# The path for overfull experts: a run-time loop with transfers on SP becomes seven conditional blocks without SP

## The chip, the cores and the metric

The kernel runs on one core of a Trainium2 chip. The metric is the device time of one launch in microseconds (us). TensorE (PE) multiplies matrices and has its own queue of weight loads (PEld); VectorE (DVE), ScalarE (ACT) and GpSimd (POOL) do the rest; SyncE (SP) here does nothing but issue transfers from HBM to the on-chip memory. A letter q behind an engine's name (SPq) marks its sequencer: register loads, branches, semaphores, issues of transfers. A measurement of this kernel can tell about 0.2% from no change.

## The reference

A trunk of two layers over 256 tokens of width 1024. Each layer has a mixer half (normalisation, an mLSTM branch and a grouped-query attention branch, merged and projected) and a half with experts, all in float32. The change concerns the second half alone. Cut down:

```python
def hierarchical_moe(h, ...):                     # h: 256 tokens x 1024
    p_group = softmax(t @ w_rg + b_rg)            # 4 groups, the best one is taken
    p_top, g_idx = lax.top_k(p_group, 1)
    ...                                           # 8 experts in each group
    w_top, e_idx = lax.top_k(p_exp, TOP_K)        # the best two of the group
    w_top = w_top / jnp.sum(w_top, ...) * p_top
    combine = ...                                 # 256 x 32, two entries in each row
    for g in range(N_GROUPS):
        a = einsum('td,edf->tef', t, w_gate[sl])  # 1024 -> 512
        u = einsum('td,edf->tef', t, w_up[sl])
        act = silu(a) * u * combine[:, sl, None]
        out = out + einsum('tef,efd->td', act, w_down[sl])   # 512 -> 1024
```

The layer then adds `gate2 * out` to its tokens. A token uses two of the 32 experts, so an expert has 16 tokens on average, and how many each has is known only at run time.

## The kernel before, in words

`experts(l, ...)` does this half for layer `l`. Logits, the choice of experts and each token's place in its expert's list (`posm`) come first; `pp[:, 64:96]` holds the count of tokens of each expert. Each expert has 64 slots (`CAP`), and the experts are worked on as 16 pairs of 2 x 64 slots (loop over `i`, L1449).

For a pair, `onehot` (L1247) compares `posm` with the slot numbers, `weigh` (L1254, GpSimd) puts the weights in, `gather` (L1263) multiplies the tokens with the one-hot matrix, `gate_up` (L1294) runs gate and up, `act_mul` and `act_T` (L1307, L1311) form and turn the activations, `down` (L1317) multiplies with the down weights, `leave` (L1332) scales and splits the result into `yh` and `yl`, and `scatter` (L1339) adds it to the tokens `xs`. The scatter of a pair is done within the next pair.

All weights stream through a ring of slots in the on-chip memory. A gate, up or down matrix of a pair comes in two pieces of 2 MB (`pump`, L173 to L208: L194 and L196 issue one whole piece, L191 two halves of 1 MB). SP issues them in an order fixed when the program is built, each when its slot is free (TensorE has read what was in it) and a completion count is free. TensorE's and SP's order is that of the program text (`MANUAL`, L64); the small work on VectorE, ScalarE and GpSimd is put in order by a planner.

After pair 11 (`MIDDLE`) the kernel provides for experts with more than 64 tokens: `rest()` (L1414). All five engines load the largest count (L1415; it is written to `ci` by L1241 to L1243 in `weights()`) and compare it with 64 (L1417). Only if it is larger does a run-time loop over the 32 experts run, load each count, and for a full expert do `rest_block` (L1379) twice, for tokens 64 to 191 and from 192 on. `rest_block` gathers 128 tokens and loads the expert's weights in eight transfers from SP into `y` (L1396, L1406), the same tile that `leave` writes. With the inputs here no expert has more than 64 tokens. Behind the `if` the next pair's `onehot`, `gather` and `turn` follow (L1478 to L1480).

Of the kernel before, what the change touches and what calls it, by code (L numbers as in the profile page):

```python
# [10 lines left out]
F32 = mybir.dt.float32  # L11
I32 = mybir.dt.int32
F32R = mybir.dt.float32r
AF = mybir.ActivationFunctionType
ALU = mybir.AluOpType
AX = mybir.AxisListType.X
PSUM = bass.MemoryType.PSUM

P = 128
S = 256  # L20
D = 1024
NT = 2
# [4 lines left out]
NE = 32  # L27
# [6 lines left out]
CAP = 64  # L34
NPAIR = NE // 2
# [25 lines left out]

PK = {"cols": (0, 96), "br": (96, 36), "gb": (132, 16), "gqk": (148, 128), "b3": (276, 8), "wg8": (284, 256)}
NPK = 540
MANUAL = {mybir.EngineType.PE, mybir.EngineType.SP}  # L64


def trunk(ctx, tc, x, c, b_ada, b_in, mlstm_norm_g, norm2_g, final_g,
          rope, gate_t, up_t, down_t, tail_t, ada_t, in_t, branch_t, out_t, packs, router, out, dbg=None, depth=DEPTH):
    nc = tc.nc
    V, A, G, T = nc.vector, nc.scalar, nc.gpsimd, nc.tensor  # L70
# [3 lines left out]
    sm = ctx.enter_context(tc.tile_pool(name="sm", bufs=2))  # L74
# [199 lines left out]
    first = {}  # L274
# [52 lines left out]
    iot = cst.tile([P, P], F32, name="iot")  # L327
    desc = cst.tile([P, 8], F32, name="desc")
    whose = cst.tile([P, 2 * NE], I32, name="whose")
# [804 lines left out]
    def experts(l, p, pL, lc, ssn, xa, sh2c):  # L1134
# [3 lines left out]
        y = pool.tile([P, D], F32, name="y")  # L1138
# [11 lines left out]
        def small(nm, *shape):  # L1150
            n = 1
            for v in shape:
                n *= v
            o = used[0]
            used[0] += n
            assert used[0] <= 1760
            return at(10, o, *shape)
# [5 lines left out]
        for t in range(NT):  # L1163
# [4 lines left out]
            if t == 0:  # L1168
                V.scalar_tensor_tensor(xp[1][:, t], xa[:, t], r, xp[0][:, t].bitcast(F32), op0=ALU.mult,
                                       op1=ALU.subtract)  # L1170
# [38 lines left out]
        pp = ps.tile([P, 512], F32, tag="c", name="pp")  # L1209
        T.matmul(pp[:, 0:64], lhsT=trisb, rhs=mk.rearrange("p t g e -> p (t g e)"), start=True, stop=False)  # L1210
        T.matmul(pp[:, 32:64], lhsT=onesb, rhs=mkf[:, 0, :], start=False, stop=True)
        for t in range(NT):
            T.matmul(pp[:, 64:96], lhsT=onesb, rhs=mkf[:, t, :], start=t == 0, stop=t == 1)
        posm = small("posm", NT, NE)
        V.scalar_tensor_tensor(posm, pp[:, 0:64].rearrange("p (t e) -> p t e", t=NT), 1.0, mkf, op0=ALU.add,
                               op1=ALU.mult)
        V.tensor_scalar(posm, posm, -1.0, None, op0=ALU.add)

        cb = small("cb", NT, NE)
        ci = sm.tile([1, NE + 1], I32, tag="ci", name="ci", bufs=1)  # L1220

        def weights():
            eg = small("eg", NT, 4)
            V.tensor_tensor(eg, lg, gm_.unsqueeze(2).to_broadcast([P, NT, 4]), op=ALU.subtract)
            A.activation(eg, eg, AF.Exp)
            e2 = small("e2", NT, 4)
            V.tensor_tensor(e2, m2, m1, op=ALU.subtract)
            A.activation(e2, e2, AF.Exp)
            sg_ = small("sgs", NT)
            V.tensor_reduce(sg_, eg, axis=AX, op=ALU.add)  # L1230
            wa, wb = small("wa", NT, 4), small("wb", NT, 4)
            V.scalar_tensor_tensor(wa, e2, 1.0, sg_.unsqueeze(2).to_broadcast([P, NT, 4]), op0=ALU.add, op1=ALU.mult)
            V.reciprocal(wa, wa)
            V.tensor_tensor(wa, wa, oh4, op=ALU.mult)
            V.tensor_tensor(wb, wa, e2, op=ALU.mult)
            V.tensor_tensor(oh1, oh1, wa.unsqueeze(3).to_broadcast([P, NT, 4, 8]), op=ALU.mult)
            V.tensor_tensor(oh2, oh2, wb.unsqueeze(3).to_broadcast([P, NT, 4, 8]), op=ALU.mult)
            V.tensor_tensor(cb, oh1.rearrange("p t g e -> p t (g e)"), oh2.rearrange("p t g e -> p t (g e)"),
                            op=ALU.add)
            mxc = small("mxc", 1)  # L1240
            V.tensor_copy(ci[:, 0:NE], pp[0:1, 64:96])  # L1241
            V.tensor_reduce(mxc[0:1, :], pp[0:1, 64:96], axis=AX, op=ALU.max)
            V.tensor_copy(ci[:, NE:NE + 1], mxc[0:1, :])  # L1243

        marks = {}

# [33 lines left out]
        count = [0]  # L1280
# [95 lines left out]
                turn_rows(range(2, 4))  # L1376


        def rest_block(e, at_, base):  # L1379
            pe = small("pe", NT, 1)  # L1380
            V.tensor_scalar(pe, posm[:, :, ds(e, 1)], -float(base), None, op0=ALU.add)
            ce = small("ce", NT, 1)
            V.tensor_copy(ce, cb[:, :, ds(e, 1)])
            oh = slots_of.rearrange("p t e s -> p (t e s)")[:, 0:S].rearrange("p (t s) -> p t s", t=NT)
            ow = same("ow", 10, 0, 2, NT, P)
            for t in range(NT):
                V.tensor_scalar(oh[:, t, :], iot, pe[:, t, :], None, op0=ALU.is_equal)
                V.tensor_scalar(ow[:, t, :], oh[:, t, :].bitcast(F32), ce[:, t, :], None, op0=ALU.mult)
            gather(oh)
            owT, wsl = turn(ow, True)  # L1390
            pgu = []
            for w in (gate_t, up_t):
                pg = ps.tile([P, 512], F32, tag="f", name="pgr")
                for h in range(4):
                    wc = y.rearrange("p (a b) -> p a b", a=2)
                    nc.sync.dma_start(wc, w[l, ds(at_[0], 1), h // 2].rearrange("o p (e k f) -> (o p) e k f", e=2, k=4)  # L1396
                                      [:, ds(at_[1], 1), 2 * (h % 2):2 * (h % 2) + 2].rearrange("p e k f -> p (e k) f"))
                    for kk in range(2):
                        T.matmul(pg, lhsT=xg[2 * h + kk][:, 0:P], rhs=wc[:, kk, :], start=h == 0 and kk == 0,
                                 stop=h == 3 and kk == 1)  # L1400
                pgu.append(pg)
            act_mul(*pgu, wsl)
            act_T()
            pd = [ps.tile([P, 512], F32, tag="f", name="pdr0"), ps.tile([P, 512], F32, tag="f", name="pdr1")]
            for k in range(4):
                nc.sync.dma_start(y, down_t[l, ds(at_[0], 1), k // 2].rearrange("o p (e k f) -> (o p) e k f", e=2, k=2)  # L1406
                                  [:, ds(at_[1], 1), k % 2].rearrange("p e f -> p (e f)"))
                for n in range(2):
                    T.matmul(pd[n], lhsT=aT[:, k, :], rhs=y[:, 512 * n:512 * n + 512], start=k == 0, stop=k == 3)
            for n in range(2):  # L1410
                leave(n, pd[n])
            scatter(owT)

        def rest():  # L1414
            full = nc.values_load(ci[0:1, NE:NE + 1], min_val=0, max_val=S,  # L1415
                                  skip_runtime_bounds_check_because="a count of at most 256 rows")
            with tc.If(full > CAP):  # L1417
                with tc.For_i(0, NE, 1) as e:
                    ne = nc.values_load(ci[0:1, ds(e, 1)], min_val=0, max_val=S,
                                        skip_runtime_bounds_check_because="a count of at most 256 rows")  # L1420
                    with tc.If(ne > CAP):
                        at_ = [nc.values_load(whose[0:1, ds(NE * v + e, 1)], min_val=0, max_val=(NPAIR - 1, 1)[v],
                                              skip_runtime_bounds_check_because="a constant table") for v in range(2)]
                        for base in (CAP, CAP + P):
                            rest_block(e, at_, base)

        nextp = None
        oh = onehot(0)
        with tc.issue_after(marks["oh"].ins):
            marks["lo"] = V.scalar_tensor_tensor(xp[1][:, 1], xa[:, 1], r, xp[0][:, 1].bitcast(F32), op0=ALU.mult,  # L1430
                                                 op1=ALU.subtract)
# [9 lines left out]
        def next_slots(i):  # L1441
            oh = onehot(i // 2)
            return oh, [weigh(i + j, oh) for j in range(2)]
# [5 lines left out]
        for i in range(NPAIR):  # L1449
            odd = i % 2 == 1  # L1450
            middle = i == MIDDLE
            pg = gate_up("wg", i)
            if turned is None:
                turned = turn(ow[0])
            owT, wsl = turned
            if i == NPAIR - 1:
                scatter_last(pend)
                pend = None
            pu = gate_up("wu", i)
            act_mul(pg, pu, wsl)  # L1460
            if odd and i + 1 < NPAIR and not middle:
                gather(oh)
            scatter_last(pend)
            if i + 1 < NPAIR and not middle:
                turned = turn(ow[(i + 1) % 2])
            act_T()
            if i == NPAIR - 1:
                if not last:
                    nc.gpsimd.dma_start(g1b, b_ada[l + 1, 2 * D:3 * D].partition_broadcast(P))
                down_last(i, owT)  # L1470
                break
            down(i)
            pend = owT
            if middle:
                scatter_last(pend)
                pend = None
                rest()
                oh, ow = next_slots(i + 1)  # L1478
                gather(oh)
                turned = turn(ow[0])  # L1480
            if not odd and i + 2 < NPAIR and i + 1 != MIDDLE:
                oh, ow = next_slots(i + 2)
            if not last and i == 3:
                nextp = params(l + 1, nc.gpsimd)
        dump(f"x{l}", xs)
# [5 lines left out]
    with tc.manual_schedule(engines=MANUAL):  # L1491
        p = setup()
        for l in range(depth):
            got = mixer(l, p)
            p = experts(l, p, *got)
# [100 lines left out]
```

## Time and profile before

| | us |
|---|---|
| median of 3 runs | 1459.84 |
| lowest and highest | 1457.97, 1459.91 |
| the profiled execution | 1458.14 |
| its span, first to last instruction | 1456.4 |
| TensorE busy in it | 1324.0 (91%) |
| VectorE, ScalarE, GpSimd busy | 615.3, 403.4, 264.5 |
| moved over the span | 521.29 MB, 358 GB/s on average |

The span falls into mixer 0, experts 0 (from about 290 us to 740 us), mixer 1 and experts 1 (from about 990 us to the end). TensorE's busy share is an average over these; a busy TensorE can be one that is paced by arriving weights, since small waits between groups of matmuls are what is left of its time. What matters for one place is which wait ends last there. "Idle before" in a row is the idle time of that engine in front of the instruction, with what ended it.

### The profile page before, as it was taken

The numbers are of one execution on the slowest core, as the hardware profiler recorded it, in microseconds if no ns is written. First come the engines' busy times: TensorE is split into PE (matmuls) and PEld (weight loads), VectorE is DVE, ScalarE is ACT, GpSimd is POOL, SyncE is SP. The second block draws the span as 40 slices with busy tenths as digits, with TensorE's granted clock in tenths as the row PEclk, the third lists the DMA queues.
The fourth block names the chain that finished last, engine by engine and source line by source line (L and its number), as shares of the span: only waits on it lengthen the run. The fifth ranks groups of instructions, "written<-read, shape, count | busy, mean of one in ns | idle before, by whom it ended". The sixth has DMA issues, their size and how long they took to land. (4 is left out here: it accounts for less than half of the span.)

```text
span 1456.4 us, 19790 instructions
## 1 busy us (share of the span) xinstructions
PE 1324.0 (91%) x7836; PEld 771.7 (53%) x7837; DVE 615.3 (42%) x1376; ACT 403.4 (28%) x755; POOL 264.5 (18%) x297
## 2 busy tenths in 40 slices
PE   6899999799999989789889999997999998987996
PEld 3788779734443434234359788893443443433432
DVE  3686756613323223212268776653323232223223
ACT  3636564411111101101046366542111111101111
POOL 2553336200000000000045533550000000000000
PEclk9999999899999999999999999998999999999998
DMA  9866594899999999999996556459999999999995
GB/s 385 350 267 251 234 366 170 329 387 424 426 427 424 425 428 425 425 384 416 424 415 239 227 188 241 178 232 370 426 425 424 428 425 425 427 425 424 373 427 231
DMA packets 50148, 521.29 MB, mean 358 GB/s; under 512 B 6656, under 2 KB 6656, under 8 KB 9344
## 3 DMA queue, kind: packets, MB, share of 16 engines
q1 hardware_dynamic: 48576, 515.94, 85.9%
q0 software_dynamic: 608, 2.14, 0.4%
q10 hardware_dynamic: 864, 1.85, 0.3%
q8 instruction: 65, 1.06, 0.3%
q14 instruction: 35, 0.29, 0.1%
HBM read 518.86 MB, written 1.05 MB: 357 GB/s over the span
## 5 line engine op out<-in xcount | busy, mean ns | idle before, releaser
L1300 PE MATMUL pgu<-arena 128*64 128x512 f32 x1376 | 325.9, 599 | 19.7 <-DMA arena<-in_gate_t_dram 12.6
L1300 PEld LDWEIGHTS pgu<-arena 128*64 128x64 f32 x1376 | 104.4, 138 | 232.1 <-issue 196.5
L1324 PE MATMUL pd<-arena 128*64 128x512 f32 x800 | 195.5, 595 | 21.8 <-ACT arena L1315 21.8
L1309 DVE SCALAR_TENSOR_TENSOR arena<-pgu,wsl,arena 128x512 f32<-128x512 f32 x32 | 24.0, 751 | 381.1 <-PE pgu L1300 381.1
L1256 POOL TENSOR_TENSOR arena<-oh,arena 128x256 f32<-128x256 f32 x32 | 19.5, 615 | 728.4 <-DVE oh L1250 465.5
L579 PE MATMUL pd<-R,R 128*128 128x256 f32 x1056 | 138.6, 290 | 3.3 <-DVE arena L619 1.7
L579 PEld LDWEIGHTS pd<-R,R 128*128 128x128 f32 x1056 | 132.3, 196 | 10.9 <-issue 6.1
L560 PE MATMUL pd<-R,R 128*128 128x256 f32 x1008 | 132.0, 289 | 4.7 <-ACT R L520 3.6
L501 POOL TENSOR_TENSOR R<-arena,R 128x512 fp32r<-128x512 f32 (+1 forms) x74 | 113.6, 1536 | 121.9 <-ACT R L520 88.7
L1324 PEld LDWEIGHTS pd<-arena 128*64 128x64 f32 x800 | 60.0, 137 | 137.5 <-issue 107.9
L560 PEld LDWEIGHTS pd<-R,R 128*128 128x128 f32 x1008 | 125.2, 194 | 13.9 <-issue 5.3
L1335 DVE TENSOR_TENSOR y<-pd,arena 128x512 f32<-128x512 f32 x64 | 44.1, 692 | 198.0 <-PE pd L1324 167.1
L1336 ACT CAST yh<-y 128x512 fp32r<-128x512 f32 x64 | 39.6, 619 | 235.5 <-DVE y L1335 235.5
L1300 PE MATMUL pgu<-B,arena 128*64 128x512 f32 x352 | 97.5, 594 | 2.3 <-DMA B<-in_up_t_dram 1.7
L501 DVE TENSOR_TENSOR R<-arena,R 128x512 fp32r<-128x512 f32 (+1 forms) x82 | 72.8, 896 | 61.1 <-ACT R L520 52.8
L1272 PE MATMUL pG<-oh,X 128*128 128x256 f32 x512 | 73.3, 306 | 16.1 <-DVE oh L1250 15.9
L1347 DVE TENSOR_TENSOR xs<-xs,psc 128x512 f32<-128x512 f32 x128 | 79.4, 681 | 17.6 <-PE psc L1344 17.6
L1272 PEld LDWEIGHTS pG<-oh,X 128*128 128x128 f32 x512 | 69.5, 211 | 27.4 <-issue 26.5
L520 ACT CAST R<-arena 128x1024 fp32r<-128x1024 f32 x66 | 68.8, 1042 | 50.1 <-PE pd L579 23.2
L1315 ACT COPY arena<-pat 128x512 f32<-128x512 f32 x32 | 18.7, 586 | 210.2 <-PE pat L1314 210.2
L1300 PE MATMUL pgu<-X,arena 128*64 128x512 f32 x320 | 72.3, 593 | 4.5 <-DMA X<-in_up_t_dram 4.5
L1308 ACT ACTIVATE arena<-pgu 128x512 f32<-128x512 f32 x32 | 19.1, 597 | 192.5 <-PE pgu L1300 192.5
(319 smaller groups left out, 1652.8 us busy)
## 6 DMA issues: line engine op xcount, KB each, us to landing
arena<-in_down_t_dram SPq DMA_DIRECT2D x45, 2048.0 KB, 29.4
arena<-in_up_t_dram SPq DMA_DIRECT2D x42, 2048.0 KB, 28.0
arena<-in_gate_t_dram SPq DMA_DIRECT2D x39, 2048.0 KB, 27.2
arena<-in_ada_t_dram SPq DMA_DIRECT2D x31, 1024.0 KB, 6.6
B<-in_up_t_dram SPq DMA_DIRECT2D x12, 2048.0 KB, 31.1
arena<-in_in_t_dram SPq DMA_DIRECT2D x23, 1024.0 KB, 6.5
X<-in_gate_t_dram SPq DMA_DIRECT2D x10, 2048.0 KB, 32.3
X<-in_up_t_dram SPq DMA_DIRECT2D x10, 2048.0 KB, 34.5
```

The source lines that it names most:

```text
L501: eng.tensor_tensor(dst, full, hi.bitcast(F32), op=ALU.subtract)
L520: A.copy(wh, w)
L560: T.matmul(acc[key][o][:, 0:S], lhsT=w[:, kk, P * o:P * o + P], rhs=x_[:, 4 * kh + kk], start=kh == 0 and i == 0 and kk == 0, stop=kh == 1 ...
L579: T.matmul(acc[key][t][:, 0:256], lhsT=x_[:, 4 * kh + kk, P * t:P * t + P], rhs=w[:, kk], start=kh == 0 and i == 0 and kk == 0, stop=kh == ...
L1256: G.tensor_tensor(ow, oh[:, :, 2 * (i % 2):2 * (i % 2) + 2].bitcast(F32), cb[:, :, 2 * i:2 * i + 2].unsqueeze(3).to_broadcast([P, NT, 2, C ...
L1272: T.matmul(pG[:, kk, 0:n], lhsT=x_[:, t, P * k:P * k + P], rhs=oh[:, t, :], start=i == 0, stop=i == 3)
L1300: T.matmul(pg[CAP * e:CAP * e + CAP, :], lhsT=xg[4 * h + kk][:, P * (i % 2) + CAP * e:P * (i % 2) + CAP * e + CAP], rhs=w[e][:, kk, :], st ...
L1309: V.scalar_tensor_tensor(ac.rearrange("p k q -> p (k q)"), pu, wsl[:, 0:1], sl, op0=ALU.mult, op1=ALU.mult)
L1324: T.matmul(pd[n][CAP * e:CAP * e + CAP, :], lhsT=aT[:, 2 * h + kk, CAP * e:CAP * e + CAP], rhs=w[e][:, kk, 512 * n:512 * n + 512], start=h ...
L1335: V.tensor_tensor(y[:, cs], pd, gt2b[:, cs], op=ALU.mult)
L1336: A.copy(yh[:, cs], y[:, cs])
L1347: V.tensor_tensor(xx, xx, pq, op=ALU.add)
```

## The change

The loop over 32 experts becomes seven blocks written out one after another, each under its own condition. VectorE works out on the chip, in pair 2 (`blocks()`), how many blocks of 128 tokens there are beyond the first 64 of any expert, and a list of the experts that they belong to, with the first token of each. At most seven can exist (`ROUNDS` = 2 x 256 // 65). The outer condition asks whether there is any block, the inner ones whether there is a block `j`.

The values are loaded only on GpSimd, ScalarE, TensorE and VectorE (`OTHERS`); SP takes no part. The eight weight transfers of a block are issued by GpSimd. In `weights()` the three operations that wrote `ci` give way to one copy of the counts.

```diff
+OTHERS = (mybir.EngineType.Pool, mybir.EngineType.Activation, mybir.EngineType.PE, mybir.EngineType.DVE)
+ROUNDS = 2 * S // (CAP + 1)
...
-            mxc = small("mxc", 1)
-            V.tensor_copy(ci[:, 0:NE], pp[0:1, 64:96])
-            V.tensor_reduce(mxc[0:1, :], pp[0:1, 64:96], axis=AX, op=ALU.max)
-            V.tensor_copy(ci[:, NE:NE + 1], mxc[0:1, :])
+            V.tensor_copy(cnt, pp[:, 64:96])
+
+        def blocks():
+
+            f = sm.tile([P, 2, NE], F32, tag="fb", name="fb", bufs=1)
+            for b in range(2):
+                V.tensor_scalar(f[:, b, :], cnt, float(CAP + P * b), None, op0=ALU.is_gt)
+            n = sm.tile([P, 1], F32, tag="nb", name="nb", bufs=1)
+            V.tensor_reduce(n, f, axis=mybir.AxisListType.XY, op=ALU.add)
+            V.tensor_copy(ci[:, 8:9], n[0:1, :])
+            ff = f.rearrange("p b e -> p (b e)")
+            V.scalar_tensor_tensor(ff, iot[:, 0:2 * NE], 1.0, ff, op0=ALU.add, op1=ALU.mult)
+            v = sm.tile([P, 8], F32, tag="vb", name="vb", bufs=1)
+            V.max(v, ff)
+            V.tensor_scalar(first_of, v, NE + 0.5, None, op0=ALU.is_gt)
+            V.scalar_tensor_tensor(v, first_of, -float(NE), v, op0=ALU.mult, op1=ALU.add)
+            V.tensor_scalar(v, v, -1.0, 0.0, op0=ALU.add, op1=ALU.max)
+            V.tensor_copy(ci[:, 0:8], v[0:1, :])
+            V.tensor_scalar(first_of, first_of, float(P), float(CAP), op0=ALU.mult, op1=ALU.add)
...
-        def rest_block(e, at_, base):
-            pe = small("pe", NT, 1)
-            V.tensor_scalar(pe, posm[:, :, ds(e, 1)], -float(base), None, op0=ALU.add)
-            ce = small("ce", NT, 1)
+        pe, ce = small("pe", NT, 1), small("ce", NT, 1)
+
+        def rest_block(e, at_, j):
+            V.tensor_scalar(pe, posm[:, :, ds(e, 1)], first_of[:, j:j + 1], None, op0=ALU.subtract)
...
-                    nc.sync.dma_start(wc, ...
+                    nc.gpsimd.dma_start(wc, ...
...
-                nc.sync.dma_start(y, ...
+                nc.gpsimd.dma_start(y, ...
...
         def rest():
-            full = nc.values_load(ci[0:1, NE:NE + 1], min_val=0, max_val=S,
-                                  skip_runtime_bounds_check_because="a count of at most 256 rows")
-            with tc.If(full > CAP):
-                with tc.For_i(0, NE, 1) as e:
-                    ne = nc.values_load(ci[0:1, ds(e, 1)], min_val=0, max_val=S,
-                                        skip_runtime_bounds_check_because="a count of at most 256 rows")
-                    with tc.If(ne > CAP):
-                        at_ = [nc.values_load(whose[0:1, ds(NE * v + e, 1)], min_val=0, max_val=(NPAIR - 1, 1)[v],
+            full = nc.values_load(ci[0:1, 8:9], engines=OTHERS, min_val=0, max_val=ROUNDS,
+                                  skip_runtime_bounds_check_because="512 rows make no more blocks")
+            with tc.If(full > 0):
+                for j in range(ROUNDS):
+                    with tc.If(full > j):
+                        e = nc.values_load(ci[0:1, j:j + 1], engines=OTHERS, min_val=0, max_val=NE - 1,
+                                           skip_runtime_bounds_check_because="the number of an expert")
+                        at_ = [nc.values_load(whose[0:1, ds(NE * v + e, 1)], engines=OTHERS[:1], min_val=0,
+                                              max_val=(NPAIR - 1, 1)[v],
                                               skip_runtime_bounds_check_because="a constant table") for v in range(2)]
-                        for base in (CAP, CAP + P):
-                            rest_block(e, at_, base)
+                        rest_block(e, at_, j)
...
+            if i == 2:
+                blocks()
```

## Rows read from the trace of the kernel before

**Rows 1.** The page, section 2: GB/s in 40 equal slices of the span.
```profile
GB/s 385 350 267 251 234 366 170 329 387 424 426 427 424 425 428 425 425 384 416 424 415 239 227 188 241 178 232 370 426 425 424 428 425 425 427 425 424 373 427 231
```

**Rows 2.** Busy times by stretch: length, five engines, PE clock, DMA share, GB/s last.
```profile
650.00:655.00 5.00, 5.00 (x26) 1.72 (x24) 0.72 (x2) 0.00 (x0) 0.00 (x0) 1.00 0.37 157
655.00:660.00 5.00, 5.00 (x26) 1.58 (x22) 1.87 (x3) 1.35 (x3) 0.00 (x0) 1.00 0.96 334
...
1355.00:1360.00 5.00, 5.00 (x26) 1.72 (x24) 0.00 (x0) 0.00 (x0) 0.00 (x0) 1.00 0.53 226
1360.00:1365.00 5.00, 5.00 (x26) 1.64 (x24) 2.59 (x4) 1.23 (x2) 0.00 (x0) 1.00 0.72 229
```

**Rows 3.** Line L1417: ns min/median/max, first and last start in us.
```profile
L1417 POOLq COMPARE_BRANCH  x2: 45/45/45, 516.9 to 1222.7; - x2
...
L1417 ACTq COMPARE_BRANCH  x2: 45/45/45, 615.4 to 1321.2; - x2
L1417 PEldq COMPARE_BRANCH  x2: 5928/6055/6182, 616.9 to 1322.6; - x2
L1417 DVEq COMPARE_BRANCH  x2: 63/68/72, 618.0 to 1323.7; - x2
L1417 SPq COMPARE_BRANCH  x2: 45/48/50, 620.7 to 1326.4; - x2
```

**Rows 4.** Timeline of SP's queue: start, us, issue (merged rows: first to last).
```profile
619.79 0.33 SPq L194 DMA_DIRECT2D arena<-in_up_t_dram  x1
...
654.34 0.33 SPq L194 DMA_DIRECT2D arena<-in_up_t_dram  x1
...
1325.70 35.15 SPq L194 DMA_DIRECT2D arena<-in_up_t_dram  x2
```

**Rows 5.** Waits around L1417 in layer 0: us in total, times, longest.
```profile
SPq L1417 <- SPq L1417: 33.4, 8, 5.1
...
DVE y L1335 <- SPq L1417: 9.3, 1, 9.3
```

**Rows 6.** Timeline behind the `if`: start, us, instruction, [idle before].
```profile
623.00 0.69 DVE L1250 TENSOR_TENSOR oh<-iot,arena 128x512 fp32r<-128x512 f32 x1 [4.39 <-PEq L1417]
...
623.84 5.55 PE L1272 MATMUL pG<-oh,X 128*128 128x256 f32 x32 [6.52 <-DVE oh L1250]
...
626.51 0.47 ACT L1276 ACTIVATE arena<-pG,sh2c 128x256 f32<-128x256 f32 x1 [11.02 <-DVE arena L1278]
...
629.54 2.79 PE L1300 MATMUL pgu<-arena 128*64 128x512 f32 x12
...
1329.00 0.69 DVE L1250 TENSOR_TENSOR oh<-iot,arena 128x512 fp32r<-128x512 f32 x1 [4.49 <-PEq L1417]
```

**Rows 7.** Timeline of PE: all waits for weights behind the `if`, both layers.
```profile
663.39 3.65 PE L1300 MATMUL pgu<-arena 128*64 128x512 f32 x16 [0.21 <-DMA arena<-in_up_t_dram]
...
692.82 3.65 PE L1300 MATMUL pgu<-X,arena 128*64 128x512 f32 x16 [1.13 <-DMA X<-in_up_t_dram]
...
707.69 3.65 PE L1300 MATMUL pgu<-arena 128*64 128x512 f32 x16 [0.62 <-DMA arena<-in_gate_t_dram]
712.51 3.65 PE L1300 MATMUL pgu<-arena 128*64 128x512 f32 x16 [1.16 <-DMA arena<-in_gate_t_dram]
...
722.57 3.65 PE L1300 MATMUL pgu<-arena 128*64 128x512 f32 x16 [0.79 <-DMA arena<-in_up_t_dram]
...
1398.88 3.65 PE L1300 MATMUL pgu<-X,arena 128*64 128x512 f32 x16 [1.06 <-DMA X<-in_up_t_dram]
...
1413.76 3.65 PE L1300 MATMUL pgu<-arena 128*64 128x512 f32 x16 [0.63 <-DMA arena<-in_gate_t_dram]
1418.57 3.65 PE L1300 MATMUL pgu<-arena 128*64 128x512 f32 x16 [1.16 <-DMA arena<-in_gate_t_dram]
...
1428.52 3.65 PE L1300 MATMUL pgu<-B,arena 128*64 128x512 f32 x16 [0.67 <-DMA B<-in_up_t_dram]
```

**Rows 8.** Line L1242: ns min/median/max of one small VectorE operation.
```profile
L1242 DVE TENSOR_REDUCE arena<-pp x2: 169/169/169, 286.1 to 991.6; 1x1 f32<-1x32 f32 x2
```

**Rows 9.** Timeline of PE before the `if`, layer 0: first and last wait for weights.
```profile
525.13 3.65 PE L1300 MATMUL pgu<-arena 128*64 128x512 f32 x16 [0.55 <-DMA arena<-in_gate_t_dram]
...
600.09 3.65 PE L1300 MATMUL pgu<-X,arena 128*64 128x512 f32 x16 [1.16 <-DMA X<-in_up_t_dram]
```

More of the change, by code (lines that the diff above doesn't have):

```diff
@@ L1219, in experts @@
         cb = small("cb", NT, NE)
-        ci = sm.tile([1, NE + 1], I32, tag="ci", name="ci", bufs=1)
+        ci = sm.tile([1, 9], I32, tag="ci", name="ci", bufs=1)
+        cnt = sm.tile([P, NE], F32, tag="cnt", name="cnt", bufs=1)
+        first_of = sm.tile([P, 8], F32, tag="first", name="first", bufs=1)
         def weights():
@@ L1395, in rest_block @@
                     wc = y.rearrange("p (a b) -> p a b", a=2)
-                    nc.sync.dma_start(wc, w[l, ds(at_[0], 1), h // 2].rearrange("o p (e k f) -> (o p) e k f", e=2, k=4)
+                    nc.gpsimd.dma_start(wc, w[l, ds(at_[0], 1), h // 2].rearrange("o p (e k f) -> (o p) e k f", e=2, k=4)
                                       [:, ds(at_[1], 1), 2 * (h % 2):2 * (h % 2) + 2].rearrange("p e k f -> p (e k) f"))
@@ L1405, in rest_block @@
             for k in range(4):
-                nc.sync.dma_start(y, down_t[l, ds(at_[0], 1), k // 2].rearrange("o p (e k f) -> (o p) e k f", e=2, k=2)
+                nc.gpsimd.dma_start(y, down_t[l, ds(at_[0], 1), k // 2].rearrange("o p (e k f) -> (o p) e k f", e=2, k=2)
                                   [:, ds(at_[1], 1), k % 2].rearrange("p e f -> p (e f)"))
```

## Prediction

> **What bounds the kernel now.** I began with the page's forty slices. In two long stretches the transfers hold 424 to 428 GB/s slice after slice [rows 1]; these are the expert halves of layers 0 and 1, where SP's queue streams 2 MB weight pieces. Take 425 GB/s as the rate at which nothing is lost. Each stretch has one dent: 384 in slice 18 and 373 in slice 38 [rows 1]. The table by 5 us stretches places them [rows 2]: 157 and 334 GB/s in 650:660, 226 and 229 in 1355:1365. Against 425 the lost time is 5 x (268 + 91) / 425 = 4.2 us in layer 0 and 5 x (199 + 196) / 425 = 4.6 us in layer 1.
>
> Next the instructions of the `if` at L1417, which stands between pairs 11 and 12. No instruction of `rest_block` appears in the trace, so no expert has over 64 rows and every engine jumps over the body. The jump itself costs ScalarE, VectorE, GpSimd and SP 45 to 72 ns, but TensorE's sequencer 5.9 to 6.2 us [rows 3]. SP's trouble comes after its jump: it issues a piece at 619.79 and the next at 654.34 [rows 4]; between them it sits 33.4 us in waits that belong to L1417 [rows 5]. Layer 1 repeats it, 35.15 us from first issue to second [rows 4]. What SP waits for must be its own transfers: the skipped body would have issued transfers and advanced their completion counts, so the arm that skips has to advance those counts in order, behind everything in flight. A 2 MB piece takes 2.097 / 0.425 = 4.9 us, so about 34.5 / 4.9 = 7 pieces are in flight, and they land one after another until about 654. Only then does SP issue again, to an empty queue. That is the dent.
>
> TensorE meanwhile restarts at 623.84, after VectorE's `oh` at 623.00, which itself waited for TensorE's jump [rows 6].
>
> **The change part by part.**
>
> *SP leaves the `if`.* The conditional values are now loaded on four engines, and the body's weight loads are GpSimd's. SP then has neither jump nor counts to advance, and its next piece waits only for a completion count and for a free slot. Pieces 12 onwards need slots that TensorE frees after the `if`, so they don't go out at 624 at once: the first follows the first half of pair 12's gate weights, read from 629.54 [rows 6] for 3.65 us (the length of sixteen such matmuls [rows 7]), hence about 633, the next ones 3.5 us apart. Each is ahead of 654, when the queue would run dry, by 20 us or so. So the transfers stay at 425 GB/s and all later pieces land 4.2 us sooner in layer 0 and 4.6 us sooner in layer 1.
>
> *What is late next.* TensorE must use that. After the `if` it runs without waiting for a piece until 663, then waits five times in layer 0 and four in layer 1, always for weights [rows 7]. A bracket of those rows understates the loss by 0.16 us: sixteen matmuls in eight pairs last 3.65 us with a last one of about 0.6, so a pair starts every 0.43 us and overlaps the next by 0.16. Layer 0: 0.21 + 1.13 + 0.62 + 1.16 + 0.79 = 3.91, plus 5 x 0.16, is 4.71 us. Layer 1: 1.06 + 0.63 + 1.16 + 0.67 = 3.52, plus 4 x 0.16, is 4.16 us. That is all TensorE can give back. In layer 0 it could reach its last up piece at 722.57 - 4.71 = 717.9, and the piece is there at 722.57 - 4.2 = 718.4: transfers still end last, gain **4.2**. In layer 1 TensorE comes at 1428.52 - 4.16 = 1424.4 and the piece at 1423.9: TensorE ends last, gain **4.16**. What follows the last piece (down, scatter, the next mixer or the output) is untouched and moves along.
>
> *Seven blocks instead of a loop with two.* Per block the code has 70 matmuls, 21 VectorE and 8 ScalarE operations. The jump of before passes 140 matmuls with their weight loads (6 us), 42 VectorE, 16 ScalarE operations and SP's 16 transfers (all under 0.1 us) [rows 3]. Now TensorE passes 490: a jump that already misses costs the same 6 us, I take no change. ScalarE passes 56: at worst 6 us from 615.4, done by 621.5, while its next work is at 626.51 [rows 6]; nothing. GpSimd's jump was at 516.9 [rows 3], over 100 us before `oh` gives it work; nothing, even with 56 transfers to pass. VectorE is the open one: 147 operations plus a load, branch and counts for each block. Its cost lies between 0.07 us (its own row) and 6.06 us (TensorE's row). At the upper end its jump, begun at 618.0, ends at 624.1 instead of just after 618, so `oh` comes at 624.2 instead of 623.00, 1.2 us later; in layer 1, from 1323.7, 0.9 us later (`oh` there is at 1329.00 [rows 6]). Below zero nothing can lie, since TensorE's jump holds `oh` anyway. I take the short jump: 147 single instructions are nearer to 42 than to the 280 and more instructions that 140 matmuls with their weight loads make, though not by much.
>
> [...]
>
> *The list of blocks.* `blocks()` adds 11 small VectorE operations per layer in pair 2; at the 169 ns of the reduce at L1242 [rows 8] about 1.9 us. Even if all of it held up TensorE once, TensorE waits for weights eight times before the `if`, from 525.13 to 600.09 in layer 0 [rows 9], brackets that add up to 9.5 us; the transfers run at full rate all that time, so it is absorbed: 0. Without that cover it would cost 1.9 a layer. `weights()` loses three operations of 0.14 to 0.17 us (L1242 is one [rows 8]) and gains a copy: between -0.3 and 0, I take 0.
>
> *Waits on `y`.* VectorE's `leave` waited 9.3 us for SP's arm [rows 5], because the body loads into `y`. GpSimd now advances these counts, early. `leave`'s results are used by the scatter of the next pair, after TensorE's piece at 663.39 [rows 7]; worth 0.
>
> **Sum.** 4.2 + 4.16 = 8.4 us. The profiled execution took 1458.14 us (span 1456.4): 1449.8 on its own time. The median of the runs, 1459.84, lies 1.7 above it, the lowest 0.2 below; so 1449.6 to 1451.5, and I write 1450.5.
>
> **The rivals.**
> *VectorE's jump misses too* (above): layer 0 gives 4.71 - 1.2 = 3.5, layer 1 4.16 - 0.9 = 3.3, sum 6.8: 1451.3 on the profiled time, 1452 as a median. For it: seven blocks are over three times the passed code. Against: 72 ns at most now.
>
> *Slots, not SP, hold the queue.* TensorE starts again 6.5 us after its last matmul before the `if` [rows 6], and slots come free that much later. If the first reissue were near 654 half of the dent would stay: gain about 4, 1454 to 1456. Against it: 633 by the rows above.
>
> *SP still takes part*, or still waits for the counts: the dent stays and the time is that of before, 1458 to 1460. For it: nothing but that the traces can't show how an engine outside an `if` is treated.
>
> [...]
>
> **How the numbers follow.** Forecast (short VectorE jump) 0.42; VectorE stall alone 0.28; slots 0.10; no effect 0.10; slower 0.08; 0.02 for a shorter jump of TensorE's, which would give the full 4.2 + 4.6 and 1449.3. The planner may also order small work on VectorE, ScalarE and GpSimd a little differently elsewhere, which I can't price from rows; it gets 2 us on the low side. Range 1447.5 to 1456.5: it leaves out no effect and slower. A measurement of this kernel tells 0.2%, 2.9 us, from no change: faster 0.82, same 0.10, slower 0.08.
>
> **What would show it.** Right: SP has no L1417 rows and issues at about 633 and then every few us; 650:660 and 1350:1360 stay above 410 GB/s; the weight waits of TensorE between the `if` and 718 shrink to nearly nothing; TensorE's jump stays near 6 us and `oh` at 623. [...] Wrong: a dent in the rate at the same place, or TensorE waiting as long for weights as before.

## The result, and the profile after

| | before | after |
|---|---|---|
| median, us | 1459.42 | 1451.45 |
| lowest and highest, us | 1457.97, 1459.91 | 1449.10, 1452.53 |
| the profiled execution, us | 1458.14 | 1452.53 |
| its span, us | 1456.4 | 1450.9 |

The ratio is 0.9945, with an interval from 0.9930 to 0.9961: 8.0 us less by the medians, where 8.4 and a time of 1450.5 had been forecast. The lines of the code shifted: the `if` is now L1437, `onehot` L1270, `gather` L1292, gate and up L1320, the turn of the activations L1334, the scatter L1364, `pump` L194 to L199.

**The dent is gone.** Section 2 of the page of the changed kernel, GB/s in 40 equal slices, against [rows 1]: slices 18 and 38 now hold 424 and 426 instead of 384 and 373.

```profile
GB/s 384 340 263 226 253 344 218 292 382 427 427 427 425 428 425 427 428 424 427 424 416 243 216 183 252 182 210 370 427 427 426 427 427 426 427 425 427 426 427 218
```

The table by 5 us stretches of the changed kernel, with the columns of [rows 2], has 424 and 429 GB/s where 157 and 334 stood, and 429 twice where 226 and 229 stood:

```profile
650.00:655.00 5.00, 4.94 (x24) 1.78 (x26) 0.00 (x0) 0.01 (x1) 0.00 (x0) 1.00 1.00 424
655.00:660.00 5.00, 5.00 (x27) 1.59 (x24) 2.67 (x4) 1.24 (x2) 0.00 (x0) 1.00 1.01 429
1355.00:1360.00 5.00, 5.00 (x26) 1.67 (x24) 2.38 (x4) 1.24 (x2) 0.00 (x0) 1.00 1.01 429
1360.00:1365.00 5.00, 5.00 (x26) 1.72 (x24) 0.29 (x1) 0.00 (x0) 0.00 (x0) 1.00 1.01 429
```

The reason stands in the timeline of SP's queue in the changed kernel (start, us from first to last of merged issues). The piece behind 622.20 goes out at 637.5 (the merged row ends 15.63 after its start), and the next two follow 3.4 us apart; in [rows 4] 34.55 us lie between one issue and the next.

```profile
622.20 15.63 SPq L197 DMA_DIRECT2D arena<-in_up_t_dram  x2
640.94 0.33 SPq L197 DMA_DIRECT2D arena<-in_down_t_dram  x1
644.37 0.33 SPq L199 DMA_DIRECT2D B<-in_down_t_dram  x1
```

**The `if` in the instructions.** Line L1437 of the changed kernel, with the columns of [rows 3]. SP has no rows, and TensorE's branch takes 5.9 to 6.1 us as before. VectorE's branch takes 63 to 72 ns as before, but the signals that follow its jump come at 625.9 when the branch was at 620.4: 5.5 us later. The stall is there; it shows behind the branch's row, not in it. GpSimd has the same gap (519.5 to 525.0), off the path.

```profile
L1437 POOLq EVENT_SEMAPHORE  x10: 17/42/43, 525.0 to 1227.2; - x10
...
L1437 PEldq EVENT_SEMAPHORE  x4: 51/51/51, 625.3 to 1327.5; - x4
L1437 DVEq EVENT_SEMAPHORE  x4: 21/21/21, 625.9 to 1327.9; - x4
L1437 POOLq COMPARE_BRANCH  x2: 45/48/50, 519.5 to 1221.3; - x2
...
L1437 PEldq COMPARE_BRANCH  x2: 5923/6022/6122, 619.3 to 1321.1; - x2
L1437 DVEq COMPARE_BRANCH  x2: 63/68/72, 620.4 to 1322.2; - x2
```

For comparison, the same signals of VectorE in the kernel before, whose branch was at 618.0 [rows 3], 0.6 us earlier:

```profile
L1417 DVEq EVENT_SEMAPHORE  x4: 21/21/21, 618.6 to 1324.7; - x4
```

**The restart.** Timeline of VectorE and TensorE behind the `if` in the changed kernel (idle before in brackets), layer 0 and layer 1, to be held against [rows 6]. `oh` is now released by VectorE's own sequencer, not by TensorE's, and TensorE stands still for 7.29 us instead of 6.52.

```profile
626.23 0.69 DVE L1270 TENSOR_TENSOR oh<-iot,arena 128x512 fp32r<-128x512 f32 x1 [5.18 <-DVEq L1437]
...
627.06 6.60 PE L1292 MATMUL pG<-oh,X 128*128 128x256 f32 x32 [7.29 <-DVE oh L1270]
...
1328.15 0.69 DVE L1270 TENSOR_TENSOR oh<-iot,arena 128x512 fp32r<-128x512 f32 x1 [5.13 <-DVEq L1437]
...
1328.98 5.65 PE L1292 MATMUL pG<-oh,X 128*128 128x256 f32 x32 [7.24 <-DVE oh L1270]
```

**What is late now.** From there to the turn in pair 15, TensorE's timeline in the changed kernel has not one wait for weights; the five and four of [rows 7] are gone. The chain of work that ended last says the same: before, its longest piece was 34.34 us of weight transfers ahead of the last up piece; now it runs back from the end over TensorE's lines to `oh` behind the `if`. Its shares by line, changed kernel:

```profile
by line: PE pgu L1320 3.8%; PE pd L1344 1.5%; PE pG L1292 0.7%; PE psc L1364 0.5%; PE pd L1385 0.4%; ACT arena L1335 0.2%; PE pat L1334 0.2%; issue 0.2%; DVE arena L1329 0.1%; DVE y L1355 0.1%; DVE yl L1357 0.1%; ACT yh L1356 0.1%; DVE xs L
```

**Where the time went.** To keep the mixers out, I measure in every kernel one interval on TensorE, from the start of the last scatter matmul before the `if` to the start of the turn (`pat`) in pair 15. Timeline of TensorE, the four ends of the kernel before:

```profile
616.94 0.39 PE L1344 MATMUL psc<-yl,owT 128*128 128x512 f32 x1
...
727.17 0.66 PE L1314 MATMUL pat<-ident,arena 128*128 128x128 f32 x4 [0.95 <-DVE arena L1309]
...
1322.84 0.39 PE L1344 MATMUL psc<-yl,owT 128*128 128x512 f32 x1
...
1433.10 0.66 PE L1314 MATMUL pat<-ident,arena 128*128 128x128 f32 x4 [0.92 <-DVE arena L1309]
```

and of the kernel after:

```profile
619.38 0.39 PE L1364 MATMUL psc<-yl,owT 128*128 128x512 f32 x1
...
726.42 0.66 PE L1334 MATMUL pat<-ident,arena 128*128 128x128 f32 x4 [0.95 <-DVE arena L1329]
...
1321.35 0.40 PE L1364 MATMUL psc<-yl,owT 128*128 128x512 f32 x1
...
1427.65 0.66 PE L1334 MATMUL pat<-ident,arena 128*128 128x128 f32 x4 [0.93 <-DVE arena L1329]
```

110.23 and 110.26 us became 107.04 and 106.30: 3.19 + 3.96 = 7.15 us. The two profiled executions differ by 5.5 us of span only, mainly because in the one of after TensorE is 2.4 us later when the first interval begins; 0.7 us of that comes back between the two intervals. It falls in the first mixer, where TensorE was granted 0.90 of its full clock in 0:70 and 0.95 in 70:140, against 0.93 and 0.99 before. That part differs from execution to execution (in after_again, the same kernel, the interval begins at 616.62 instead of 619.38), so the intervals are the better measure of the mechanism, and the medians of the change's worth.

### The profile page after: what moved, and what is told of

It is laid out like the page before. It is cut to its first block, busy times and chain, and to the rows that moved or that the text cites. A ratio compares the mean times of both kernels' runs of the same rounds, so it can differ in the third digit from the quotient of the medians.

```text
span 1450.9 us, 19793 instructions
## 1 busy us (share of the span) xinstructions
PE 1320.5 (91%) x7836; PEld 771.0 (53%) x7836; DVE 618.7 (43%) x1393; ACT 403.5 (28%) x754; POOL 263.8 (18%) x297
## 3 DMA queue, kind: packets, MB, share of 16 engines
HBM read 518.86 MB, written 1.05 MB: 358 GB/s over the span
## 5 line engine op out<-in xcount | busy, mean ns | idle before, releaser
L1320 PE MATMUL pgu<-arena 128*64 128x512 f32 x1376 | 324.7, 599 | 15.2 <-DMA arena<-in_gate_t_dram 9.6
L1320 PEld LDWEIGHTS pgu<-arena 128*64 128x64 f32 x1376 | 104.2, 138 | 226.1 <-issue 202.3
L1320 PE MATMUL pgu<-B,arena 128*64 128x512 f32 x352 | 97.4, 593 | 1.7 <-DMA B<-in_up_t_dram 1.1
L1292 PE MATMUL pG<-oh,X 128*128 128x256 f32 x512 | 74.0, 308 | 17.5 <-DVE oh L1270 17.3
L1292 PEld LDWEIGHTS pG<-oh,X 128*128 128x128 f32 x512 | 70.2, 214 | 28.8 <-issue 28.0
L1320 PE MATMUL pgu<-X,arena 128*64 128x512 f32 x320 | 72.2, 593 | 2.0 <-DMA X<-in_up_t_dram 2.0
L1296 ACT ACTIVATE arena<-pG,sh2c 128x256 f32<-128x256 f32 x64 | 30.4, 475 | 152.6 <-DVE arena L1298 150.8
```

Of the source, the lines that this page charges most:

```text
L1292: T.matmul(pG[:, kk, 0:n], lhsT=x_[:, t, P * k:P * k + P], rhs=oh[:, t, :], start=i == 0, stop=i == 3)
L1296: A.activation(xg[k][:, 0:n], pG[:, kk, 0:n], AF.Identity, bias=sh2c[:, k:k + 1])
L1320: T.matmul(pg[CAP * e:CAP * e + CAP, :], lhsT=xg[4 * h + kk][:, P * (i % 2) + CAP * e:P * (i % 2) + CAP * e + CAP], rhs=w[e][:, kk, :], st ...
```

## The experiments

One table first; the intervals are worked out from the same rows of each kernel's timeline, and a ratio is one of all the runs with its 95% interval, not the quotient of the two medians. The kernels from sp_back to blocks2 ran on one chip, beside a median of before of 1457.4 us, those from after_again to mid7 on another, beside 1457.9; each ratio is to the runs beside it.

| kernel | median, us | ratio to before | interval, layer 0 | layer 1 |
|---|---|---|---|---|
| before | 1459.42 | 1 | 110.23 | 110.26 |
| the changed kernel | 1451.45 | 0.9945 (0.9930 to 0.9961) | 107.04 | 106.30 |
| sp_back | 1457.90 | 1.0005 (0.9994 to 1.0016) | 109.36 | 109.62 |
| sp_jumps | 1450.29 | 0.9941 (0.9923 to 0.9959) | 107.19 | 106.03 |
| loop_gp | 1451.73 | 0.9965 (0.9954 to 0.9977) | 107.24 | 107.23 |
| blocks2 | 1449.69 | 0.9942 (0.9921 to 0.9963) | 106.98 | 106.27 |
| after_again | 1450.09 | 0.9939 (0.9924 to 0.9953) | 107.27 | 106.19 |
| blocks1 | 1448.47 | 0.9926 (0.9908 to 0.9944) | 105.81 | 105.46 |
| no_if | 1448.14 | 0.9925 (0.9907 to 0.9943) | 105.54 | 105.56 |
| mid7 | 1449.39 | 0.9933 (0.9918 to 0.9948) | the `if` stands elsewhere | |

**1. sp_back: seven blocks, but their transfers on SP again.**

```diff
-OTHERS = (... Pool, Activation, PE, DVE)
+OTHERS = (... Pool, Activation, PE, DVE, SP)
-                    nc.gpsimd.dma_start(wc, ...
+                    nc.sync.dma_start(wc, ...
-                nc.gpsimd.dma_start(y, ...
+                nc.sync.dma_start(y, ...
-                        at_ = [nc.values_load(..., engines=OTHERS[:1], ...
+                        at_ = [nc.values_load(..., engines=OTHERS[4:], ...
```

> Seven blocks as in the changed kernel, but SP loads the values, takes the jump and would issue the blocks' transfers, as before the change. Theory (SP's counts queue behind all transfers in flight): a gap of over 30 us between two issues of SP behind the condition, the rate falls to under 350 GB/s in two neighbouring 5 us stretches of each layer (4.2 to 4.7 us lost in each), and the time is that of the kernel before, 1458 to 1460 (VectorE's later restart hides in the dent). Rival (the gain came from the list of blocks or from the loop's disappearance): no dent, 1451.

Measured: a ratio of 1.0005; the whole gain is gone, with the blocks in place. The intervals stay 0.9 and 0.6 us under those of before, which the ratio can't tell from nothing. The table by stretches of sp_back shows the dent where it was, though the second stretch of layer 0, at 364, is over the 350 that I had expected:

```profile
650.00:655.00 5.00, 5.00 (x27) 1.60 (x24) 0.92 (x2) 0.32 (x1) 0.00 (x0) 1.00 0.35 121
655.00:660.00 5.00, 5.00 (x26) 1.71 (x24) 1.75 (x3) 0.92 (x2) 0.00 (x0) 1.00 0.92 364
1355.00:1360.00 5.00, 5.00 (x26) 1.72 (x24) 0.50 (x1) 0.00 (x0) 0.00 (x0) 1.00 0.27 115
1360.00:1365.00 5.00, 5.00 (x26) 1.64 (x24) 2.08 (x4) 1.23 (x2) 0.00 (x0) 1.00 0.89 321
```

and its SP queue (start, us) again has two issues 34.4 us apart around it:

```profile
619.39 34.76 SPq L198 DMA_DIRECT2D arena<-in_up_t_dram  x2
```

The `if` line of sp_back has SP's short jump and, behind it, nine signals in each layer that go on until 1359.4 in layer 1, 33.8 us after the branch at 1325.6. In layer 0 each of the eight signals behind the first comes within 0.1 us of the landing of a piece that was in flight (the pieces land at 629.1, 634.0, 638.9, 643.8, 646.3, 648.8 and 653.6), the last two together behind the last piece:

```profile
L1438 SPq EVENT_SEMAPHORE  x18: 17/17/17, 625.9 to 1359.4; - x18
...
L1438 SPq COMPARE_BRANCH  x2: 50/50/50, 620.3 to 1325.6; - x2
```

So neither the blocks nor the list bring the gain; taking SP's part out does. Which part of it is the next question.

**2. sp_jumps: SP jumps along, but issues none of the blocks' transfers.**

```diff
-OTHERS = (... Pool, Activation, PE, DVE)
+OTHERS = (... Pool, Activation, PE, DVE, SP)
```

> SP loads the values and takes the jump, but GpSimd issues the blocks' transfers, so SP has no completion counts to advance. Theory: no dent, SP's next issue follows within some 12 to 16 us as in the changed kernel, 1450 to 1453. Rival (SP's part in the condition, its load and jump or a meeting of the engines, is what stops the queue): the dent is back, 1458 to 1460.

Measured: 0.9941, intervals as in the changed kernel, no dent (428 and 436, 436 and 426 GB/s in the four stretches). SP's rows at the `if` of sp_jumps: the jump, and one signal 0.2 us later.

```profile
L1438 SPq COMPARE_BRANCH  x2: 45/48/50, 622.3 to 1324.3; - x2
L1438 SPq EVENT_SEMAPHORE  x2: 17/17/17, 622.5 to 1324.4; - x2
```

SP's jump costs nothing that times or intervals show. What cost it the 34 us were the completion counts of the transfers that the skipped code would have issued: 18 signals with the transfers on SP, two without. The step of the prediction that inferred this from SP's waits [rows 5] is shown.

**3. loop_gp: the kernel before, with only the loop's transfers moved to GpSimd.**

```diff
-                    nc.sync.dma_start(wc, ...
+                    nc.gpsimd.dma_start(wc, ...
-                nc.sync.dma_start(y, ...
+                nc.gpsimd.dma_start(y, ...
```

> The kernel before with one edit: GpSimd issues the transfers inside the loop; loop, five engines and two blocks stay. Theory: the whole gain is there with this edit alone: no dent, and since VectorE passes only two blocks, its jump stays short and TensorE's gap in front of the gather is 6.5 to 6.6 us instead of 7.3; 1449.5 to 1452. Rival (seven conditional blocks were needed for it): 1458 to 1460.

Measured: 0.9965, and no dent (426, 429, 423 and 426 GB/s). This one move, two words of the diff, makes the larger part of the gain; the seven blocks are not needed for it. In the loop VectorE has 42 operations to pass and its signals come 0.6 us after the branch, as in the kernel before:

```profile
L1417 DVEq EVENT_SEMAPHORE  x4: 21/21/21, 620.6 to 1322.5; - x4
...
L1417 DVEq COMPARE_BRANCH  x2: 63/68/72, 620.0 to 1321.6; - x2
```

By that alone loop_gp should have come out at or ahead of the changed kernel. It lies behind instead, by 1.4 us by the medians of the same chip (sp_jumps) and by 0.24%, 3.5 us, by the ratios, whose intervals overlap by little. About 1 us of it stands in the interval of layer 1, and in TensorE's timeline of loop_gp, where the last up piece is waited for again:

```profile
721.57 3.65 PE L1300 MATMUL pgu<-arena 128*64 128x512 f32 x16 [0.39 <-DMA arena<-in_up_t_dram]
...
1423.38 3.65 PE L1300 MATMUL pgu<-B,arena 128*64 128x512 f32 x16 [1.10 <-DMA B<-in_up_t_dram]
```

The landing times, worked out from the trace's transfers, show one piece late in each layer behind the `if` (716.60 and 1418.41) that comes 6.45 us behind its predecessor instead of 4.9. blocks2 (below) has such a piece too, in layer 0 alone. In loop_gp the late piece accounts for the interval: no_if (below), where none falls behind the `if`, needs 105.5 us, and 1.55 more is 107.1, against 107.24 and 107.23 here. The changed kernel has such pieces only ahead of the `if` (the later ones at 587.96 and 1294.83), where the interval doesn't count them, so the intervals of the two kernels don't compare like with like. The same records show what moved meanwhile: one packet of 16 KB on a queue that the page calls instruction (q8), in loop_gp at 714.01 and 1415.82, in the changed kernel at 585.81 and 1292.68, ahead of the two pieces just named, which came 5.9 us behind their predecessors. Most such packets make no piece late (between 330 and 735 us of the changed kernel 16 of them move, and three pieces come over 5.5 us behind their predecessors), and no run tests the link. What the ratios say beyond that 1 us stays open.

**4. blocks2: two blocks instead of seven.**

```diff
-ROUNDS = 2 * S // (CAP + 1)
+ROUNDS = 2
```

> The changed kernel with two blocks instead of seven (it would leave out blocks three to seven). Theory (VectorE's late restart is a fetch behind a jump over seven blocks): VectorE's signals follow its jump within 0.3 us, one-hot waits for TensorE's jump, TensorE's gap is 6.5 to 6.6 us instead of 7.3, and the time is 1 to 2 us under that of the changed kernel. Rival (the late restart comes from elsewhere, the list or the fewer engines): the gap stays 7.2 to 7.3 us.

Measured: 0.9942 against the 0.9941 and 0.9939 of seven blocks: no gain, where 1 to 2 us had been expected. VectorE's stall does go away; line L1437 of blocks2:

```profile
L1437 DVEq EVENT_SEMAPHORE  x4: 21/21/21, 619.4 to 1321.3; - x4
...
L1437 DVEq COMPARE_BRANCH  x2: 56/64/72, 618.7 to 1320.3; - x2
```

and the time that TensorE stands still falls to 6.97 and 6.66 us, by 0.3 and 0.6. TensorE's own jump of 6.2 to 6.4 us remains, so no more comes out of it. The intervals are within 0.3 us of those of seven blocks, but for two reasons. Timeline of TensorE in blocks2:

```profile
625.01 5.39 PE L1292 MATMUL pG<-oh,X 128*128 128x256 f32 x32 [6.97 <-DVE oh L1270]
...
720.03 3.65 PE L1320 MATMUL pgu<-arena 128*64 128x512 f32 x16 [1.24 <-DMA arena<-in_up_t_dram]
...
1326.47 6.13 PE L1292 MATMUL pG<-oh,X 128*128 128x256 f32 x32 [6.66 <-DVE oh L1270]
```

In layer 1 the gather, 6.13 us instead of 5.65, takes back what the shorter stop gave. In layer 0 stop and gather together are 1.5 us shorter, and TensorE then waits for the last up piece, the late one named above; without that wait the interval would be about 105.6. So VectorE's stall is real, but what it is worth isn't settled by blocks2: nothing in layer 1, and in layer 0 something that a late piece hides.

**5. blocks1: one block.**

```diff
-ROUNDS = 2 * S // (CAP + 1)
+ROUNDS = 1
```

> The changed kernel with a single block (it would leave out blocks two to seven): TensorE's jump passes 70 matmuls with their weight loads instead of 140 or more. If the 6 us are a fetch of code that lies too far ahead, this jump may be short: under 0.2 us, TensorE's gap 1 to 2 us instead of 6.5 to 7.3, the gather 4.1 to 4.5 us instead of 5.4 to 6.6, and the time that of the kernel without the condition. Rival (TensorE pays 6 us for any jump): jump 6 us, gap 6.5 us, time as with two blocks.

Measured: 0.9926, intervals of 105.81 and 105.46. With 70 matmuls to pass, TensorE's jump is short too, if not under the 0.2 us of the expectation. Line L1437 of blocks1:

```profile
L1437 PEldq COMPARE_BRANCH  x2: 323/340/358, 617.9 to 1319.9; - x2
```

340 ns over 70 matmuls stand against 5.9 to 6.4 us over 140 (before, loop_gp, blocks2) and 5.9 to 6.6 over 490 (the kernels with seven blocks): the step lies between 70 and 140, and 490 cost hardly more than 140. TensorE stands still for 2.49 and 2.46 us, more than the 1 to 2 expected. In layer 1 a part of the stall seems only to move behind the `if`: in the timeline of blocks1 the gather breaks off in its middle for 1.02 us in which the engine waits for nothing that the profile shows.

```profile
1326.20 2.17 PE L1292 MATMUL pG<-oh,X 128*128 128x256 f32 x16 [1.02 <-issue]
```

**6. no_if: no condition at all.**

```diff
                 pend = None
-                rest()
                 oh, ow = next_slots(i + 1)
```

> The changed kernel with the condition and its blocks left out (overfull experts are not served). It shows what the condition still costs. Theory (after the change TensorE's stop at the condition, 7.3 us and a slow gather, makes TensorE the last one to the end of each layer, 1.5 to 2 us behind the weights): without it the transfers end each layer, TensorE waits for weights again before the last up piece, and the time is 1.5 to 3.5 us under the changed kernel's, ratio to the kernel before 0.992 to 0.994. Rival (the transfers were the bound again already): same time as the changed kernel within 1 us and no more waits for weights.

Measured: 0.9925, intervals of 105.54 and 105.56. The gather follows the scatter at once and takes 4.0 us. Now TensorE runs into the weights again, seven times in each layer, the last time at the last up piece. Timeline of TensorE in no_if:

```profile
615.97 3.99 PE L1292 MATMUL pG<-oh,X 128*128 128x256 f32 x32
...
716.68 3.65 PE L1320 MATMUL pgu<-arena 128*64 128x512 f32 x16 [0.52 <-DMA arena<-in_up_t_dram]
...
1418.87 3.65 PE L1320 MATMUL pgu<-B,arena 128*64 128x512 f32 x16 [0.51 <-DMA B<-in_up_t_dram]
```

So 105.5 us is what the transfers need. blocks1 comes to within 0.3 us of it with a stop of 2.5 us, and it too waits for the last up piece in both layers (0.50 and 0.58 us): the short stop is covered, the long one of seven blocks is not, and costs 107.27 - 105.54 = 1.7 and 106.19 - 105.56 = 0.6 us beside it on the same chip. By the medians the whole condition still costs 1450.09 - 1448.14 = 1.95 us; the two ratios' intervals overlap.

**7. mid7 and after_again: the condition four pairs earlier, beside the changed kernel.**

```diff
-MIDDLE = 11
+MIDDLE = 7
```

> The changed kernel with the condition after pair 7 instead of pair 11 (one constant). Theory: TensorE's stop of 7.3 us then lies ahead of the stretch in which TensorE waits for weights (9.5 us of waits before pair 11, 4 to 5 us after it), so it is made up by the end, the last up piece is waited for again, and the time is that without the condition, 1.5 to 3.5 us under the changed kernel. Rival (transfers starve, because TensorE is already late there and frees slots later): a stretch under 400 GB/s behind the condition and no gain, or a loss of some us.

> The changed kernel itself, beside the others on one chip: ratio 0.993 to 0.996, VectorE's signals 5 to 5.6 us behind its jump in both layers, no dent.

The changed kernel repeats itself: 0.9939, intervals of 107.27 and 106.19, the same 5.5 us between VectorE's branch (617.7) and its signals (623.2), no wait for weights behind the `if`. With the stop behind pair 7, TensorE stands still just as long (7.57 and 7.49 us), but has four more pairs in which to catch up. It does; the last up piece is late again. Timeline of TensorE in mid7:

```profile
721.76 3.65 PE L1320 MATMUL pgu<-arena 128*64 128x512 f32 x16 [0.51 <-DMA arena<-in_up_t_dram]
...
1420.70 3.65 PE L1320 MATMUL pgu<-B,arena 128*64 128x512 f32 x16 [0.54 <-DMA B<-in_up_t_dram]
```

Those are the waits of no_if at the same place, so the stop is absorbed. The median is 0.7 us under that of the changed kernel, the intervals of the ratios overlap almost wholly: the mechanism shows in the rows, a gain in time isn't resolved. Of the kernels that provide for any number of full experts it has the lowest median.

## Why the prediction was right, and where not

- **SP's counts make the dent: right.** Shown by sp_back, sp_jumps and loop_gp together. By the rates the dent was put at 4.2 and 4.6 us; no_if, where nothing but transfers sets the end, is 110.23 - 105.54 = 4.7 and 110.26 - 105.56 = 4.7 us faster. Against that the sum over two 5 us stretches was 0.5 short in layer 0 and 0.1 in layer 1.
- **The next piece at about 633, then every 3.5 us: right in kind.** It went out behind the first half of pair 12's gate weights, as said, but these were read from 633.81 on instead of 629.54 [rows 6], so at 637.5. Of the 4.3 us, 2.4 lie ahead of the `if`, 1.8 in the longer stand and the longer gather. The next two follow 3.4 us apart, and the queue didn't run dry.
- **TensorE can give back 4.71 and 4.16: right.** All nine waits went. In layer 0 the forecast had transfers end last; in fact TensorE did in both layers.
- **VectorE's jump is short: wrong.** This is the step that failed, and the first rival (chance 0.28) is what happened. I judged by the nearest row, 42 operations in 72 ns, and looked at the branch's own row, where a stall of VectorE doesn't show: it stayed at 63 to 72 ns, with 5.5 us behind it. `oh` came 6.85 us after the last scatter matmul instead of 6.06 in layer 0, and 6.80 instead of 6.16 in layer 1: 0.8 and 0.6 us later, where the rival had 1.2 and 0.9. That a jump over 147 operations stays as short as one over 42 was my estimate from that one row; no run shows it, and the first signal came 5.5 us after the branch over 147 and 0.7 us after it over 42 (blocks2), in layer 0.
- **The gather behind the stop: a term that I left out.** In layer 0 it took 6.60 us instead of 5.55 [rows 6]; in layer 1 5.65 where the kernel before has 5.78; no_if has 4.0. Timeline of TensorE in the kernel before, layer 1:

```profile
1329.84 5.78 PE L1272 MATMUL pG<-oh,X 128*128 128x256 f32 x32 [6.61 <-DVE oh L1250]
```

TensorE's granted clock goes from 1.00 to 0.50 within the stop and back to 1.00 within the gather. In the changed kernel the trace has it at 0.50 from 622.6 to 632.8 and from 1325.7 to 1332.6, in the kernel before from 620.4 to 627.2 and from 1326.9 to 1333.7. So 5.7 and 3.6 us of the gather ran at 0.50, against 3.4 and 3.9 before; counted at half, which is an estimate from these shares, all four gathers come to 3.7 to 3.9 us, about the 4.0 of no_if, which has no stop and is granted 1.00 in the three stretches from 623 to 641. By that estimate the longer gather of layer 0 is the clock coming back later. Repetitions of the same kernel vary (6.77 and 5.39 in after_again, behind stops of 7.34 and 7.38), so it isn't the length of the stop alone that decides when. The table by stretches of the changed kernel, granted clock third from the end of a row:

```profile
623.00:629.00 6.00, 1.94 (x9) 1.97 (x10) 0.69 (x1) 0.00 (x0) 1.19 (x2) 0.50 0.99 416
629.00:635.00 6.00, 6.00 (x33) 5.13 (x34) 2.75 (x7) 1.90 (x4) 0.00 (x0) 0.68 1.01 425
635.00:641.00 6.00, 6.00 (x30) 2.00 (x28) 0.44 (x1) 0.00 (x0) 0.61 (x1) 1.00 1.00 423
```

- **The sum with these terms.** Layer 0: 4.71 - 0.77 (longer stand) - 1.05 (longer gather) = 2.89, measured 3.19. Layer 1: 4.16 - 0.63 + 0.13 = 3.66, measured 3.96. The 0.3 left in each would follow if the overlap of two pairs of matmuls were a little over the 0.16 us per wait that I took; this was not tried. Together 7.15 us, nearer to the rival's 6.8 than to my 8.4. That the median came within 1 us of the forecast is partly luck: the runs scatter by some 3 us, and the 8.0 us of the medians is more than these intervals give.
- **The list of blocks, `weights()` and the wait on `y` at nothing: nothing speaks against it.** The eight waits before the `if` in layer 0 add up to 9.45 us after and 9.53 before [rows 9].
- **Slower (0.08): didn't happen.** Two stalls of 6 us one after the other could have made it so, but VectorE's and TensorE's overlap: first signals at 625.9 and 625.3, not 6 us apart. With 4.71 us to give back in layer 0, the change would have been slower there from a restart of 623.84 + 4.71 - 616.94 = 11.6 us after the last scatter matmul; it came after 627.06 - 619.38 = 7.7.

## What to carry to other kernels

An engine whose queue of transfers is full shouldn't own transfers in a branch that is almost never taken: skipping it here waited for everything in flight, 34 us and 4.7 us of the layer's time, while GpSimd, with nothing in flight, skipped such transfers for nothing that the end sees (from 330 to 726 us only SP's q1 and the two instruction queues move packets in the changed kernel). Code that was passed over wasn't free here either, up to 6.6 us for TensorE and 5.9 for VectorE: look for the price in the gap between the branch and the next instruction of that engine, for each engine. And a stop that can't be avoided belongs where enough work follows for the engine to meet its next wait again; mid7's rows show that, its time doesn't resolve it.

## What the runs showed of the hardware that was not expected

- The jump of TensorE took 0.32 to 0.36 us over 70 matmuls with their weight loads, and 5.9 to 6.6 us over 140 or 490; VectorE's first signal came 0.6 to 0.7 us after its branch over 42 operations, and 5.5 to 5.9 us over 147 (layer 0).
- On VectorE and GpSimd this stall lies behind the branch's row (rows of 63 to 72 and 45 to 50 ns in the changed kernel, first signals 5.5 us later in layer 0), on TensorE in it (5.92 to 6.12 us).
- TensorE and VectorE, which stall at the same `if` in the changed kernel, stall side by side (619.3 to 625.3 and 620.4 to 625.9 in layer 0), with transfers at 419 to 421 GB/s in the 5 us stretches of the changed kernel between 620 and 630 and between 1320 and 1330.
- Section 3 of the page lists two queues of the kind instruction. The second (q14) moved 41 packets in the changed kernel, 35 in the kernel before, 32 in blocks1 and 30 in no_if. By the trace's records one 16 KB packet of the first (q8) moves between TensorE's branch and its first signal in both layers of the kernel before (from 620.19 and 1326.27) and of the changed kernel (622.66 to 623.68, and from 1324.66), and none in blocks1. Between VectorE's branch and its first signal two 8 KB packets of the second queue move in the changed kernel (621.35 and 623.90 in layer 0, 1323.47 and 1325.83 in layer 1), and none in the kernel before and in blocks2. The expectations of blocks1 and blocks2 call the stalls fetches; that they are waits for these packets is a reading that no run tests.
